# The FFN and its second products: six head units, units in pairs, operand sets in the order of use, outputs added from PSUM

## The chip, the cores and the metric

The kernel runs on one core of a Trainium2 chip. The time is the device time of one execution, in microseconds. Each core has five engines with instruction streams of their own that meet only through semaphores: PE (matrix products; its weight loads are shown as PEld), DVE (vector), ACT (activation), POOL (GpSimd) and SP, which here only issues DMAs.

## The reference

A block over a sequence of 1024 tokens with 1024 channels: a mixer (a gated convolution and a state-space scan, merged), then a SwiGLU feed-forward network (FFN), each behind a normalization that is shifted and scaled by a condition, then a last normalization.

```python
def ffn_sublayer(h, w_ffn_in, w_ffn_down):
    gate, up = jnp.split(h @ w_ffn_in, 2, axis=-1)
    return (jax.nn.silu(gate) * up) @ w_ffn_down
...
x = x + gate * mixer_sublayer(h, ...)
shift, scale, gate = adaln(c, w_ada_ffn[i], b_ada_ffn[i])
h = rms_norm(x, norm_ffn_w[i]) * (1.0 + scale) + shift
x = x + gate * ffn_sublayer(h, w_ffn_in[i], w_ffn_down[i])
return rms_norm(x, final_norm_w)
```

D_FF is 2816, so the FFN has 22 blocks of 128 gate and up columns.

## The kernel before

Channels lie on partitions (blocks of 128) and tokens in two halves of 512. Every fp32 operand is split into a high and a low part (`split`, `wsplit`): ACT writes the high part, then DVE or POOL subtracts it from the raw value for the low part. A product of four blocks is 12 matmuls (`mmp`, line 804).

Large products are done by units. A unit multiplies a 2x2 arrangement of weight blocks (two output blocks by two halves of the input channels) by a 2x2 arrangement of activations (two channel halves by the two token halves) in seven products instead of eight, as Strassen and Winograd do. The weights of products a to g are two blocks as they are, four combinations (`fs`, and three made in place, lines 901 to 906) and one more block. The activations are seven operand sets of four blocks each, made once for all units by `tok_ops`: B11 and B21 are the tiles H of the first token half as they stand; T1 to T4 and B22 come from `b2` (the second half), `t1` and `b21` (the first half, summed on POOL again from the parts of H by `whole`). `Unit.first` does the products a and b, which need only H. `Unit.rest` does the other five, in the order T1, T2, B22, T3, T4. Three accumulators take them: X, Y, Z in PSUM.

Three stages matter here:
- The FFN (`ffn_in`, 22 units, names `f0` to `f21`): `second` loads the second half, `tok_ops` normalizes it and makes the sets while the first `FF_HEAD` = 4 units do their products a and b. From then on a unit's `first` stands beside the `rest` of the one before. Results go to DRAM (`act_d`).
- The second products (`down_both(q)`, q = 0 and 1, four units each, names `d00` to `d13`): the same scheme on eight blocks of `act_d`; sets first, four `first`, then four `rest`. `Down.done` loads a block of x from DRAM (`pv`, two buffers), adds the product times the gate and stores it.
- The remainder (`down_rest`): six blocks without units, the last normalization, and the output.

The letters of `ENG_A`, `ENG_F`, `ENG_D` give the engine (v DVE, g POOL) of a unit's seven weight splits and its four weight combinations, for the first units and then for all others. Weight blocks arrive in 512 KB DMAs (`load_unit`: the first block of a unit in the tag `wraw`, the second in `fraw`, two buffers each). A head unit's first block is loaded twice: once for `first`, once for `rest`. The order on each engine is made by a scheduler from the order of the code and its own estimate of times; each engine, SP's queue among them, then works strictly in that order.

Of the kernel before, what the change touches and what calls it, by code (L numbers as in the profile page):

```python
# [14 lines left out]
P = 128  # L15
# [13 lines left out]
FF_HEAD = 4  # L29
FF_TAIL = 2  # L30
D_NEXT = 1
# [42 lines left out]
def build(tc, ins, outs):  # L74
# [208 lines left out]
    def bcast(colsr, name, far=True):  # L283
# [16 lines left out]
        bcast.last = last.ins  # L300
# [31 lines left out]
    row_d = dram.tile([24, NCK, P], F32, name="row_d")  # L332
    H = [tuple(hpool.tile([P, T], F32R, name=f"H{q}{k}") for q in "hl") for k in range(KD)]

    def make_h(k, t, gcol, shift, r, eng, dst=H):
        vec.scalar_tensor_tensor(out=t, in0=t, scalar=gcol[:, k:k + 1], in1=r, op0=ALU.mult, op1=ALU.mult)
        hi, lo = dst[k]
        act(out=hi, in_=t, func=AF.Identity, bias=shift[:, k:k + 1])
        if eng is vec:
# [446 lines left out]
    def load_unit(*cs):  # L786
        t = []
        for c in cs:
            if c != cs[0]:
                w = pools["u"].tile([P, 8 * P], F32, tag="fraw", name=f"fw{c}", bufs=2)  # L790
# [29 lines left out]
    def tok_ops(pool_, b2, t1, norm):  # L820
# [12 lines left out]
        for k in range(4):  # L833
            whole(t1[k], k)
# [14 lines left out]
        for k in range(4):  # L849
            less(k, t1[k])  # L850
            bsp("T1", k, t1[k], vec)
        for k in range(4):
            less(4 + k, t1[k])
            bsp("T2", k, t1[k], vec)
            bsp("B22", k, b2[4 + k], gp)
        for k in range(4):
            gp.tensor_tensor(out=b2[k], in0=b2[4 + k], in1=b2[k], op=ALU.subtract)
            bsp("T3", k, b2[k], vec)
        for k in range(4):
            b21 = tmp(f"b21_{k}")  # L860
            whole(b21, 4 + k)
# [17 lines left out]
    class Unit:  # L879


        def __init__(self, name, i, cons, four, engs):
            self.name, self.i, self.cons, self.four, self.engs = name, i, cons, four, engs

        def first(self, raw):
            n, e = self.name, self.engs
            self.raw = raw if len(raw) == 4 else None
            self.X = xtile(self.i, f"uX{n}") if self.four else mmtile(f"uX{n}")
            Y = pstile(f"uY{n}")
            mmp(self.X, wsplit(raw[0], f"a{n}", e[0]), BO["B11"])  # L890
            s1 = self.cons.tile11()
            act(out=s1, in_=self.X, func=AF.Copy)
            mmp(Y, wsplit(raw[1], f"b{n}", e[1]), BO["B21"])
            self.cons.c11(s1, Y)

        def rest(self, raw):
            n, e, X = self.name, self.engs, self.X
            a11, a12, a21, a22 = raw or self.raw
            tick()
            s1 = pools["u"].tile([P, T], F32, tag="fs", name=f"fs{n}", bufs=1)  # L900
# [3 lines left out]
            e[9].tensor_tensor(out=a11, in0=s1, in1=a11, op=ALU.subtract)  # L904
            w2 = wsplit(a11, f"d{n}", e[3])
            e[10].tensor_tensor(out=a12, in0=a12, in1=a11, op=ALU.subtract)
            Z = pstile(f"uZ{n}")
            mmp(Z, w1, BO["T1"])
            s5 = ev(f"s5{n}")
            act(out=s5, in_=Z, func=AF.Copy)  # L910
            mmp(X, w2, BO["T2"], False)
            s2 = ev(f"s2{n}")
            act(out=s2, in_=X, func=AF.Copy)
            mmp(Z, wsplit(a12, f"e{n}", e[4]), BO["B22"], False)
            self.cons.c12(s2, Z)
            mmp(X, wsplit(a21, f"f{n}", e[5]), BO["T3"], False)
            self.cons.c22(s5, X)
            mmp(X, wsplit(a22, f"g{n}", e[6]), BO["T4"], False)
            self.cons.c21(X)
# [4 lines left out]
    def run_units(name, units, HEAD, TAIL, four, engs, pre, after):  # L924
# [9 lines left out]
        def p37(i, load):  # L934
            step(U[i].rest, units[i][:2] if load else None)
            for f in after.get(i, ()):
                step(f)
# [3 lines left out]
        for i in range(HEAD - 1):  # L941
            p37(i, True)
        for i in range(HEAD, N - TAIL):
            p12(i, True)
            p37(i - 1, i == HEAD)
# [5 lines left out]
        for i in range(N - TAIL, N):  # L951
            p37(i, True)


    class Each:
# [23 lines left out]
    class ConvIn:  # L979
        def __init__(self, i):  # L980
            self.i = i
# [46 lines left out]
    class SsmIn:  # L1028
# [45 lines left out]
    def phase_a():  # L1074
# [38 lines left out]
        def begin(_):  # L1113
            popen("a1", "a1")
            pools["u"], pools["nev"] = mp, 6
            pt = [pools["c"].tile([P, NH * T + CW - 1], F32, tag="u", name=f"t1_{k}", bufs=2) for k in range(2)]
            t1 = [pt[k // 2][:, k % 2 * T:(k % 2 + 1) * T] for k in range(4)]
            tok_ops(pools["a1"], x1t, t1, norm_of(x1t, r_row, gmix, mod_m[:, 0:8]))
# [551 lines left out]
```

## Time and profile before

| what | value |
|---|---|
| runs | 2179.09, 2188.5, 2185.9 us (median 2185.9) |
| the profiled execution | 2181.88 us, span 2180.2 us |
| busy: PE, DVE, POOL, ACT | 1969.9, 1600.5, 1271.0, 974.0 us |
| granted clock of TensorE, mean | 0.957 |
| moved by DMA | 360.71 MB |

In the profile one instruction of a group is named by line, engine, operation and tile: L213 is the low part of an activation split, L783 that of a weight split, L804 a product's matmul, L922 the addition of a product to an SBUF tile, L1404 the addition to `pv`. Buffer numbers are left out of names. In the 40 slices a digit is the busy share in tenths, and a slice is 54.5 us; the first is slice 0.

### The profile page before, as it was taken

What the parts mean: (1) busy time and instruction counts of PE and PEld (TensorE: products, weight loads), DVE (VectorE), ACT (ScalarE), POOL (GpSimd) and SP (SyncE); (2) the same over time, 40 slices, a digit from 0 to 9 for tenths busy, and PEclk for the clock granted to TensorE, in tenths of its full rate; (3) what the DMA queues carried; (4) which work ended last, traced back from release to release, by engine and by line L of the source; (5) the groups of instructions that cost most, each with busy time, mean ns of one, the idle gap of its engine ahead of it and who ended that gap; (6) DMA issues with size and microseconds to landing.
All of it is one profiled execution on the core that took longest, in us unless ns stands there. A gap on an engine that the chain in (4) does not pass through costs nothing.

```text
span 2180.2 us, 26745 instructions
## 1 busy us (share of the span) xinstructions
PE 1969.9 (90%) x8802; PEld 1558.0 (71%) x8802; DVE 1600.5 (73%) x2195; ACT 974.0 (45%) x1814; POOL 1271.0 (58%) x938
## 2 busy tenths in 40 slices
PE   3889999999999797999889899977999999978997
PEld 3668678787877566777677687755888888756775
DVE  8878889968897979778688955567544345797845
ACT  3544344444446656545554542344333333443443
POOL 4668668878875755576555755565333334665411
PEclk9999999999999898999999999987999999999898
DMA  8223222323227866877888777742222222545663
GB/s 313 88 82 104 87 76 97 115 87 105 99 83 236 260 214 192 289 250 258 267 292 281 231 236 258 234 151 82 83 79 80 87 83 97 169 164 181 201 215 114
DMA packets 161227, 360.71 MB, mean 165 GB/s; under 512 B 18440, under 2 KB 18880, under 8 KB 161088
## 3 DMA queue, kind: packets, MB, share of 16 engines
q1 hardware_dynamic: 161088, 359.00, 49.6%
q8 instruction: 69, 1.13, 0.2%
q14 instruction: 70, 0.57, 0.1%
HBM read 275.80 MB, written 83.13 MB: 165 GB/s over the span
## 4 chain that ended last, share of the span: by engine, by line
PE 47%; DVE 24%; DMA 14%; issue 5%; ACT 2%; POOL 2%; SPq 1%; DVEq 0%; POOLq 0%; ACTq 0%
PE uXp L804 11%; PE uXf L804 10%; PE uZp L804 6%; PE uZf L804 4%; PE uYp L804 3%; DMA wa_f<-in 2%; PE uYf L804 2%; DMA M<-acs_d 2%; DMA x_d<-pv 1%; DVE wa_f L244 1%; DMA yl<-y_d 1%; PE p L182 1%; DVE gc L1045 1%; PE p L183 1%; DVE pcM L659 1%
## 5 line engine op out<-in xcount | busy, mean ns | idle before, releaser
L168 POOL TENSOR_TENSOR wl<-w,wh 128x512 fp32r<-128x512 f32 x198 | 285.4, 1451 | 221.0 <-ACT wh L166 176.9
L166 ACT ACTIVATE wh<-w 128x512 fp32r<-128x512 f32 x232 | 136.7, 606 | 122.4 <-DMA w<-in 59.7
L547 ACT ACTIVATE M<-M,dt_acs 128x128 f32<-128x128 f32 x256 | 80.9, 389 | 41.9 <-DMA M<-acs_d 41.8
L552 POOL TENSOR_TENSOR M<-M,cbm 128x512 f32<-128x512 f32 x48 | 68.8, 1443 | 48.0 <-ACT M L549 43.9
L659 DVE SCALAR_TENSOR_TENSOR pcM<-u,cw_eo,pcM 128x512 f32<-128x512 f32 x120 | 90.2, 752 | 2.7
L659 DVE SCALAR_TENSOR_TENSOR pcQ<-u,pc,pcQ 128x512 f32<-128x512 f32 x112 | 84.4, 753 | 3.0
L659 DVE SCALAR_TENSOR_TENSOR pcR<-u,pc,pcR 128x512 f32<-128x512 f32 x104 | 78.4, 754 | 2.8
L183 PE MATMUL s<-Hl,wh 128*128 128x512 f32 x192 | 77.2, 403 | 3.7 <-DVE Hl L213 3.7
L184 PE MATMUL s<-Hh,wl 128*128 128x512 f32 x192 | 77.7, 406 | 2.4 <-POOL wl L168 2.4
L182 PE MATMUL s<-Hh,wh 128*128 128x512 f32 x192 | 77.2, 406 | 0.1
L182 PE MATMUL p<-Hh,wh 128*128 128x512 f32 x144 | 59.1, 430 | 19.6 <-DVE xo L1026 10.8
L182 PE MATMUL p<-Oh,wh 128*128 128x512 f32 x144 | 60.7, 421 | 10.8 <-DVE xo L1026 10.8
L922 DVE TENSOR_TENSOR s2f<-s2f,uZf 128x512 f32<-128x512 f32 x22 | 15.1, 686 | 73.9 <-PE uZf L804 73.9
L183 PE MATMUL p<-Hl,wh 128*128 128x512 f32 x144 | 60.2, 419 | 6.0 <-DVE Hl L340 5.9
L901 POOL TENSOR_TENSOR fsf<-fw 128x512 f32<-128x512 f32 x22 | 34.9, 1588 | 50.4 <-DVE cf3l L783 3.3
L903 DVE TENSOR_TENSOR fw<-fw,fw 128x512 f32<-128x512 f32 x31 | 47.3, 1525 | 22.9 <-POOL fsf L901 19.0
L183 PE MATMUL p<-Ol,wh 128*128 128x512 f32 x144 | 59.9, 416 | 0.0
L184 PE MATMUL p<-Oh,wl 128*128 128x512 f32 x144 | 59.4, 414 | 0.0
L184 PE MATMUL p<-Hh,wl 128*128 128x512 f32 x136 | 56.7, 417 | 0.0
L1023 DVE SCALAR_TENSOR_TENSOR p<-pre,pc,p 128x512 f32<-128x512 f32 x72 | 53.8, 747 | 1.1 <-ACT p L1019 0.5
L244 DVE CUSTOM_DVE_ANT_0 wa_f<-wa_f,rw,as_f 128x512 f32<-128x512 f32 x24 | 31.3, 1302 | 29.9 <-DMA wa_f<-in 29.8
L184 PE MATMUL wo<-Oh,wl 128*128 128x512 f32 x128 | 50.6, 398 | 2.2 <-POOL wl L168 2.2
(3626 smaller groups left out, 7188.6 us busy)
## 6 DMA issues: line engine op xcount, KB each, us to landing
fw<-in SPq DMA_DIRECT2D x131, 512.0 KB, 3.4
w<-in SPq DMA_DIRECT2D x100, 512.0 KB, 4.9
M<-acs_d SPq DMA_DIRECT2D x64, 256.0 KB, 6.5
wa_f<-in SPq DMA_DIRECT2D x48, 256.0 KB, 3.9
wa_m<-in SPq DMA_DIRECT2D x16, 512.0 KB, 10.2
xs<-xbc_d SPq DMA_DIRECT2D x32, 256.0 KB, 4.6
E<-eac_d SPq DMA_DIRECT2D x64, 128.0 KB, 6.0
y<-z_d SPq DMA_DIRECT2D x32, 256.0 KB, 5.7
```

Source lines behind the costliest of these rows:

```text
L166: act(out=hi[:, :n], in_=raw, func=AF.Copy)
L168: eng.tensor_tensor(out=lo[:, :n], in0=raw, in1=hi[:, :n].bitcast(F32), op=ALU.subtract)
L182: nc.tensor.matmul(out=out, lhsT=whi[:, sl], rhs=rh, start=first and i == 0, stop=False)
L183: nc.tensor.matmul(out=out, lhsT=whi[:, sl], rhs=rl, start=False, stop=False)
L184: nc.tensor.matmul(out=out, lhsT=wlo[:, sl], rhs=rh, start=False, stop=last and i == n - 1)
L244: vec.tensor_tensor_reduce(out=w, in0=w, in1=c, scale=1.0, scalar=first, op0=ALU.mult, op1=ALU.add, accum_out=o)
L547: act(out=m[:, sl], in_=m[:, sl], func=AF.Relu, scale=-1.0, bias=acs[:, c * 32 + hd:c * 32 + hd + 1])
L552: (gp if e or hf == 0 else vec).tensor_tensor(out=self.M[e], in0=self.M[e], in1=cbm, op=ALU.mult)
L659: vec.scalar_tensor_tensor(out=pt if k < n - 1 else out or pt, in0=src(k), scalar=w(k), in1=pt, op0=ALU.mult, op1=ALU.add)
L804: nc.tensor.matmul(out=out, lhsT=l[:, sl], rhs=r, start=first and k == 0 and i == 0, stop=k == 3 and i == 2, skip_group_check=True)
L903: e[8].tensor_tensor(out=a21, in0=a11, in1=a21, op=ALU.subtract)
L1023: vec.scalar_tensor_tensor(out=pt, in0=pre[:, k:k + T], scalar=wc(k), in1=pt, op0=ALU.mult, op1=ALU.add)
```

## The change

- `FF_HEAD` is 6. The X of units 4 and 5 are taken from the PSUM tiles of Y and Z.
- Units go in pairs: `rest` is a generator that stops after each product, and `rests` takes a product of one unit and then of the other. The head's six units make three pairs, the last two units of the FFN one, and the units of `down_both` two per q. After each round `more_ops` makes the next operand set, so that the sets stand in the code between the products that use them.
- In these two stages B22 and the difference for T3 are made on DVE. The first half's blocks are not summed from H: in the FFN, phase B writes four of them to `t1f` with one more ACT instruction each, and `b21` is still summed; in `down_both` all eight are loaded from `act_d`.
- In the head units and in `down_both` all seven weight splits are on DVE and the four combinations on POOL.
- `Down` adds each product from PSUM straight into `pv` (`p1` to `p7`); the blocks of x are loaded when the unit's part begins. There are eight buffers for `pv` (tag `g0`).
- The last scaling of a half reads the broadcast row from PSUM on DVE; two of eight blocks stay on POOL.

```diff
-FF_HEAD = 4
+FF_HEAD = 6
-D_NEXT = 1
-N_PV = 2
+N_G0 = 8
-G_GP = 6
-ENG_F = ("ggggggggvvv", "ggvgvgvgvvv")
-ENG_D = ("gvvgggggvvv", "ggvgvgvgvvv")
+ENG_F = ("vvvvvvvgggg",) * 6 + ("ggvgvgvgvvv",)
+ENG_D = ("vvvvvvvgggg",)
...
     def make_h(...)
         act(out=hi, in_=t, func=AF.Identity, bias=shift[:, k:k + 1])
+        if keep is not None:
+            act(out=keep, in_=t, func=AF.Identity, bias=shift[:, k:k + 1])
...
     def tok_ops(...)
         for k in range(4):
             less(k, t1[k])
             bsp("T1", k, t1[k], vec)
+        yield
         for k in range(4):
             less(4 + k, t1[k])
             bsp("T2", k, t1[k], vec)
-            bsp("B22", k, b2[4 + k], gp)
+        yield
         for k in range(4):
-            gp.tensor_tensor(out=b2[k], in0=b2[4 + k], in1=b2[k], op=ALU.subtract)
+            bsp("B22", k, b2[4 + k], other)
+        yield
+        for k in range(4):
+            other.tensor_tensor(out=b2[k], in0=b2[4 + k], in1=b2[k], op=ALU.subtract)
             bsp("T3", k, b2[k], vec)
+        yield
...
+    def more_ops(gen=None):
+        if gen:
+            ops_left[:] = [gen]
+        if ops_left and next(ops_left[0], ops_left) is ops_left:
+            ops_left.clear()
+
+    def rests(us, raw):
+        gens = [u.rest(raw and raw[4 * i:4 * i + 4]) for i, u in enumerate(us)]
+        while gens:
+            gens = [g for g in gens if next(g, gens) is not gens]
+            more_ops()
...
     class Down:
-        def done(self, src, m, hf):
+        def begin(self, part):
+            for m, hf in ((0, 0),) if part == 0 else ((1, 1), (0, 1), (1, 0)):
+                t = self.t[m, hf] = pools["u"].tile([P, T], F32, tag="g0", ..., bufs=N_G0)
+                dma(out=t, in_=x1_d[hf, m + 2 * self.u])
+
+        def add(self, src, m, hf, last):
+            t = self.t[m, hf]
             m += 2 * self.u
-            t = pools["d0"].tile([P, T], F32, tag="pv", name=f"pv{self.q}{hf}_{m}", bufs=N_PV)
-            dma(out=t, in_=x1_d[hf, m])
             vec.scalar_tensor_tensor(out=t, in0=src, scalar=mod_f[:, 16 + m:17 + m], in1=t, op0=ALU.mult, op1=ALU.add)
-            dma(out=x1_d[hf, m], in_=t)
-
-        def c11(self, s1, Y):
-            add(s1, s1, Y)
-            self.done(s1, 0, 0)
+            if last:
+                dma(out=x1_d[hf, m], in_=t)
+
+        def p1(self, X):
+            self.add(X, 0, 0, False)
+
+        def p2(self, Y):
+            self.add(Y, 0, 0, True)
...
-                        (gp if k % 3 == 1 else vec).tensor_tensor(out=o, in0=o, in1=r, op=ALU.mult)
+                        (gp if k % 4 == 1 else vec).tensor_tensor(out=o, in0=o, in1=r if k % 4 == 1 else bcast.row,
+                                                                  op=ALU.mult)
```

How instructions move is seen at three places. First POOL at the head of the FFN, before, from the first split of a `df` on:

```order
L783 TENSOR_TENSOR df0l<-fw_12623,df0h 128x512
L783 TENSOR_TENSOR ef0l<-fw_12623,ef0h 128x512
L783 TENSOR_TENSOR ff0l<-fw_12625,ff0h 128x512
L857 TENSOR_TENSOR b2f_12350<-b2f_12358,b2f_12350 128x512
L213 TENSOR_TENSOR B22l_12417<-b2f_12358,B22h_12416 128x512
L857 TENSOR_TENSOR b2f_12352<-b2f_12360,b2f_12352 128x512
L783 TENSOR_TENSOR gf0l<-fw_12625,gf0h 128x512
```

The same engine there now, from the sums for `b21` on (`fsf` and `fw` are the weight combinations of units 0 and 1):

```order
L833 TENSOR_TENSOR b_0_12882<-Hh_111,Hl_112 128x512
L833 TENSOR_TENSOR b_1_12889<-Hh_113,Hl_114 128x512
L916 TENSOR_TENSOR fsf_12660<-fw_12608 128x512
L918 TENSOR_TENSOR fw_12608<-fw_12606,fw_12608 128x512
L919 TENSOR_TENSOR fw_12606<-fsf_12660,fw_12606 128x512
L925 TENSOR_TENSOR fw_12606<-fw_12606 128x512
L916 TENSOR_TENSOR fsf_12683<-fw_12612 128x512
```

Splits, B22 and T3's differences have left POOL, and the combinations, of which only `fs` was here, have come.

Second DVE at the start of q=0, before, where it takes in the first unit's products (`dg`, `uYd`):

```order
L922 TENSOR_TENSOR dg_15809<-dg_15809,uYd_15792 128x512
L862 TENSOR_TENSOR td_0_15677<-b_0_15761,td_0_15677 128x512
L838 TENSOR_TENSOR td_2_15679<-b2d_6_15673,td_2_15679 128x512
L213 TENSOR_TENSOR T2l_15716<-td_1_15678,T2h_15715 128x512
L1404 SCALAR_TENSOR_TENSOR pv_0_15828<-dg_15809,mod_f,pv_0_15828 128x512
```

And now:

```order
L784 TENSOR_TENSOR ad01l<-fw_15700,ad01h 128x512
L211 TENSOR_TENSOR T2l_15936<-t1f_99,T2h_15935 128x512
L1478 SCALAR_TENSOR_TENSOR pv_0_15703<-uXd_15702,mod_f,pv_0_15703 128x512
L784 TENSOR_TENSOR bd01l<-fw_15700,bd01h 128x512
L873 TENSOR_TENSOR t1f_99<-b_4_16098,t1f_99 128x512
L842 TENSOR_TENSOR t1f_100<-b2d_5_15670,t1f_100 128x512
L865 TENSOR_TENSOR b2d_1_15662<-b2d_5_15670,b2d_1_15662 128x512
```

The product goes from `uXd` into `pv` in one instruction, and weight splits (L784) and T3's differences (L865) stand between the sets' rows.

Third SP's queue in q=0, before, around a unit's reload of weights (`fw`):

```order
L793 DMA fw_15875<-in 128x1024
L1405 DMA x_d<-pv_0_15828 128x512
L1350 DMA act_d<-g_21_15312 128x512
L1403 DMA pv_4_15914<-x_d 128x512
L793 DMA fw_15918<-in 128x1024
L1405 DMA x_d<-pv_2_15871 128x512
```

And now, between the reloads for the first unit and for the second:

```order
L794 DMA fw_15823<-in 128x1024
L1473 DMA pv_2_15908<-x_d 128x512
L1430 DMA b2d_0_16396<-act_d 128x512
L1511 DMA b_7_16119<-act_d 128x512
L1430 DMA b2d_1_16398<-act_d 128x512
L1511 DMA b_4_16834<-act_d 128x512
L1430 DMA b2d_2_16400<-act_d 128x512
L1430 DMA b2d_3_16402<-act_d 128x512
L794 DMA fw_15827<-in 128x1024
```

Loads of the next q's second half (`b2d` with numbers from 16396, which take the buffers of this q's `b2d`) and of `b21` now stand ahead of the second unit's reload.

More of the change, by code (lines that the diff above doesn't have):

```diff
@@ L299, in bcast @@
                                     rhs=ident, start=True, stop=True, skip_group_check=True)
-        bcast.last = last.ins
+        bcast.last, bcast.row = last.ins, pr
         t = stp.tile([P, T], F32, tag="st", name="bc" + name)
@@ L818, in build, with tok_ops @@
     BO = {}
-    def tok_ops(pool_, b2, t1, norm):
+    def tok_ops(pool_, b2, t1, norm, first=None, other=gp):
         BO.update(B11=H[0:4], B21=H[4:8], T1=[], T2=[], T3=[], T4=[], B22=[])
@@ L831, in whole @@
             gp.tensor_tensor(out=t, in0=H[k][0].bitcast(F32), in1=H[k][1].bitcast(F32), op=ALU.add)
-        for k in range(4):
-            whole(t1[k], k)
+        if first is None:
+            for k in range(4):
+                whole(t1[k], k)
         def less(k, t):
@@ L854, in tok_ops @@
             bsp("T2", k, t1[k], vec)
-            bsp("B22", k, b2[4 + k], gp)
+        yield
         for k in range(4):
-            gp.tensor_tensor(out=b2[k], in0=b2[4 + k], in1=b2[k], op=ALU.subtract)
+            bsp("B22", k, b2[4 + k], other)
+        yield
+        for k in range(4):
+            other.tensor_tensor(out=b2[k], in0=b2[4 + k], in1=b2[k], op=ALU.subtract)
             bsp("T3", k, b2[k], vec)
+        yield
         for k in range(4):
-            b21 = tmp(f"b21_{k}")
-            whole(b21, 4 + k)
+            b21 = first and first(4 + k)
+            if not b21:
+                b21 = tmp(f"b21_{k}")
+                whole(b21, 4 + k)
             vec.tensor_tensor(out=t1[k], in0=b21, in1=t1[k], op=ALU.subtract)
@@ L932, in p12, with p37 @@
             step(U[i].first, units[i][:2] if whole else units[i][:1])
[L934 to L937, printed above, removed]
+        def p37(n, load):
+            us = n if isinstance(n, tuple) else (n,)
+            step(lambda raw: rests([U[i] for i in us], raw), sum((units[i][:2] for i in us), ()) if load else None)
+            for i in us:
+                for f in after.get(i, ()):
+                    step(f)
         for i in range(HEAD):
             p12(i, False)
-        for i in range(HEAD - 1):
-            p37(i, True)
+        if pairs:
+            for i in range(0, HEAD, 2):
+                p37((i, i + 1), True)
+        else:
+            for i in range(HEAD - 1):
+                p37(i, True)
         for i in range(HEAD, N - TAIL):
             p12(i, True)
-            p37(i - 1, i == HEAD)
+            if i > HEAD or not pairs:
+                p37(i - 1, i == HEAD)
         for i in range(N - TAIL, N):
@@ L950, in run_units @@
             step(pre)
-        for i in range(N - TAIL, N):
-            p37(i, True)
-    class Each:
+        for i in range(N - TAIL, N, 2):
+            p37((i, i + 1), True)
+    class Each(Sums):
         def __init__(self, name, done):
@@ L1357, in second @@
             dma(out=b2[k], in_=src[k0 + k])
-        return b2, [pools["d0"].tile([P, T], F32, tag="d", name=f"t{name}_{k}", bufs=4) for k in range(4)]
+        return b2
     def act_load(hf, i, hl):
@@ L1370, in begin @@
             popen("cv", "cv", space=PSUM)
[L1371 removed]
             fp = popen("f", "f")
[L1373 to L1374 removed]
+            pools.update(u=fp, nev=8, nfr=4, nfs=1)
+            b2 = second(x1_d[1], 0, "f")
             r = bcast(r_x1[1], "x1f1", far=False)
[L1376 removed]
+            more_ops(tok_ops(fp, b2, t1f, norm_of(b2, r, gffn, mod_f[:, 0:8], KD, True), lambda k: None, vec))
             bg_ada.append(late(ADA_LATE, ada(None, wada_ffn, range(8, 12), mod_f, gffn, "f")))
@@ L1426, in down_both, with first @@
         ch = lambda m: CH_FD + 3 * m + q
+        def first(k):
+            t = tmp(f"b21_{k}")
+            dma(out=t, in_=act_d[0, KD * q + k])
+            return t
         def begin(_):
-            b2, t1 = second(act_d[1], KD * q, f"d{q}")
-            tok_ops(pools["u"], b2, t1, None)
+            b2 = second(act_d[1], KD * q, f"d{q}")
+            for k in range(4):
+                dma(out=t1f[k], in_=act_d[0, KD * q + k])
+            more_ops(tok_ops(pools["u"], b2, t1f, None, first, vec))
         def pre(_):
@@ L1441, in down_both @@
             step(U[u].first, units[u][:1])
-        for u in range(4):
-            step(U[u].rest, units[u])
-            if u == D_NEXT:
+        for u in range(0, 4, 2):
+            step(lambda raw, u=u: rests(U[u:u + 2], raw), units[u] + units[u + 1])
+            if u == 0:
                 step(pre)
```

135 lines of the change are left out of this document (78 added, 57 removed).

## The prediction

> **What bounds the kernel now.** I read the page first (engine totals, then the slices), next stretches of the second half, then who waited for whom in the slow stretches, then single instructions there.
>
> ```profile
> span 2180.2 us, 26745 instructions
> PE 1969.9 (90%) x8802; PEld 1558.0 (71%) x8802; DVE 1600.5 (73%) x2195; ACT 974.0 (45%) x1814; POOL 1271.0 (58%) x938
> PE   3889999999999797999889899977999999978997
> DVE  8878889968897979778688955567544345797845
> POOL 4668668878875755576555755565333334665411
> DMA  8223222323227866877888777742222222545663
> ```
>
> PE is the busiest engine, but in the last third its row dips three times (slices 27 and 28, then 35 to 38), and in each dip DVE rises to 8 or 9 and POOL to 5 or 6. The dips are the head of the FFN (1428 to 1510 us) and the two second products, q=0 and q=1 (1880 to 2095). A table of stretches gives their size (columns: busy time and starts of PE, weight loads, DVE, ACT, POOL; granted clock; DMA share; GB/s):
>
> ```profile
> 1436.20:1446.20 10.00, 2.86 (x13) 2.02 (x12) 9.55 (x12) 1.14 (x3) 9.36 (x8) 0.75 0.96 353
> 1449.00:1500.40 51.40, 37.67 (x123) 26.12 (x121) 48.48 (x45) 28.86 (x50) 35.04 (x22) 0.74 0.09 31
> 1525.00:1850.00 325.00, 325.00 (x1420) 266.17 (x1419) 145.22 (x189) 121.59 (x204) 118.55 (x87) 1.00 0.25 85
> 1888.00:1950.00 62.00, 46.54 (x183) 35.69 (x182) 61.56 (x58) 26.97 (x49) 47.91 (x29) 0.92 0.45 156
> 1999.00:2043.00 44.00, 32.23 (x112) 23.57 (x111) 43.21 (x44) 20.55 (x38) 30.98 (x20) 0.81 0.45 150
> 1880.00:2094.60 214.60, 184.91 (x750) 144.69 (x749) 172.19 (x186) 82.72 (x149) 110.68 (x69) 0.94 0.57 190
> ```
>
> From 1525 to 1850 PE is never idle: 325.0 us for 1420 matmuls, 0.229 us each. That is the price of a matmul when nothing is late, and the change can win nothing there. From 1449 to 1500 only 123 matmuls start where 224 would fit, and DVE is busy 48.5 of 51.4 us. In 1888 to 1950 and 1999 to 2043 DVE is busy 61.6 of 62 and 43.2 of 44. So DVE bounds the dips.
>
> The instructions of the products alone (line 804):
>
> ```profile
> 1427.00:1496.00 69.00, 43.76 (x144) 30.79 (x145) 0.75 0.31 107
> 1496.00:1525.00 29.00, 26.11 (x107) 20.81 (x107) 0.94 0.37 115
> ```
>
> 251 of them from 1427.8 (the first) to 1525.0 are worth 57.5 us; with 3.5 us for the sums of squares and the broadcast the head loses 97.2-57.5-3.5 = 36 us. From 1880 to 2094.6, 750 matmuls are worth 171.7 us: the second products lose 43 us. Who PE waits for, in the head (three rows) and in q=0 (five):
>
> ```profile
> PE bx1f L298 <- DVE r_x L278: 7.3, 1, 7.3
> PE uXf L804 <- DVE T2l L213: 6.7, 3, 3.8
> PE uZf L804 <- DVE T1l L213: 6.2, 3, 3.0
> PE uZd L804 <- ACT cd01h L781: 3.5, 1, 3.5
> PE uYd L804 <- ACT bd02h L781: 3.1, 1, 3.1
> PE uXd L804 <- POOL dd00l L783: 1.7, 1, 1.7
> PE uZd L804 <- DVE cd00l L783: 1.7, 1, 1.7
> PE uZd L804 <- POOL ed00l L783: 1.4, 1, 1.4
> ```
>
> **The price of a DVE instruction.** It has two values:
>
> ```profile
> 1478.15 1.75 DVE L213 TENSOR_TENSOR T2l<-tf,T2h 128x512 fp32r<-128x512 f32 x1
> 1472.61 1.71 POOL L857 TENSOR_TENSOR b2f<-b2f,b2f 128x512 f32<-128x512 f32 x1
> 1887.74 1.28 DVE L838 TENSOR_TENSOR td<-b2d,td 128x512 f32<-128x512 f32 x2
> 1436.93 4.98 POOL L831 TENSOR_TENSOR tf<-Hh,Hl 128x512 f32<-128x512 f32 x4
> L1404 DVE SCALAR_TENSOR_TENSOR pv<-dg,mod_f,pv 128x512 f32<-128x512 f32 x8 | 10.4, 1301 | 0.0
> L1404 DVE SCALAR_TENSOR_TENSOR pv<-uXd,mod_f,pv 128x512 f32<-128x512 f32 x6 | 4.5, 749 | 7.6 <-PE uXd L804 6.7 <-DMA pv<-x_d 0.8
> ```
>
> Alone it takes 0.6 us from start to start (two in 1.28, the last one's tail included); beside a POOL instruction 1.75. The same instruction costs 1.30 with both tensors in SBUF, 0.75 with one in PSUM. What a POOL instruction adds comes from three stretches, as DVE's busy time less 0.6 per instruction: (48.5-45x0.6)/22 = 0.98, (61.6-58x0.6)/29 = 0.92, (43.2-44x0.6)/20 = 0.84. I take 0.92. The Trainium skill, "SBUF — State Buffer", section "SBUF: two separate sides", says that DVE with two SBUF inputs and GpSimd hold a shared port pair in turn, for the whole instruction. The trace agrees in kind. By that rule the charge would be POOL's whole 1.25 us (four in 4.98): 0.33 more on 13 and 20 instructions counted below, 11 us in all, so 2141 us instead of my sum; the three stretches decide for 0.92.
>
> **The change, part by part.**
>
> *Head of the FFN, set-up.* Before the sets can be made, twelve small DVE instructions (`rsqrt`) run from 1436.2 to 1446.2, beside POOL (9.36 us busy in the stretch quoted). At the end of the program the same chain runs without POOL, and there are the rows that set when set-making starts:
>
> ```profile
> 2164.84 0.16 DVE L270 TENSOR_SCALAR vx<-scx 128x4 f32<-128x4 f32 x1 [2.48 <-PE scx L259]
> 2167.02 0.16 DVE L278 SCALAR_TENSOR_TENSOR rx<-tx,rx 128x4 f32<-128x4 f32 x1
> 1449.04 0.75 DVE L872 SCALAR_TENSOR_TENSOR b2f<-b2f,gffn,bcx1f 128x512 f32<-128x512 f32 x1 [2.86 <-ACT bcx1f L302]
> 1452.45 0.63 ACT L781 ACTIVATE bf3h<-fw 128x512 fp32r<-128x512 f32 x1 [3.45 <-PE uYf L804]
> 1418.55 0.72 ACT L338 ACTIVATE Hh<-xh_x1f,mod_f 128x512 fp32r<-128x512 f32 x1 [4.89 <-DVE xh_x1f L336]
> fw<-in SPq DMA_DIRECT2D x131, 512.0 KB, 3.4
> ```
>
> Alone it is 2.3 us. The change takes POOL's four sums of H away from this place (phase B keeps them in `t1f`) and moves POOL's splits to DVE; two of POOL's other instructions still overlap it. I take 4.5 us for the chain, so the broadcast comes some 5 us earlier. DVE cannot use all of that: in its new order `bf3l` stands ahead of the first row of the sets, and `bf3h` waits for a weight buffer that the first Y frees. Set-making starts at about 1447 in place of 1449. The four kept copies are ACT instructions of 0.72 us in phase B, 2.9 us on an engine busy 45% of the span; taken at nothing, at worst 3.
>
> *Head of the FFN, sets.* From the first scaled `b2` to the last low part of T4 stand 62 DVE rows now (45 before, in 51.4 us), with 13 POOL instructions (22 before): 62x0.6 + 13x0.92 + 1 for the longer form = 50 us, to 1497. B22's and T3's work and all splits now stand on DVE, and the four weight sums of a unit on POOL. So the last set is ready only 3 us earlier than before. The gain is what PE has done by then. Two more units give it four more products, and each set feeds two products: its order has 242 product matmuls ahead of the first that waits for T4, where 144 had been started by 1496 before (row above). PE is through these at about 1498.5; that is 70.7 us for 55.4+3.5 us of work. With 2 us for the joints behind, the head loses 14 in place of 36: a gain of 22, which is also about what the 98 matmuls more are worth (98x0.229). Ends: 8, if DVE keeps the mean of the stretch, 48.5/45 = 1.08 us (62 rows, 67 us, 17 later); 30, if POOL's charge all but falls away (62x0.6, 1485).
>
> The next two pairs need ten products, 27.5 us of PE, against 18 DVE rows and 8 POOL ones, 18 us; a reload of a weight block (3.4 us) follows the fifth product's split and has 16 us before it is needed. Taken at nothing. From unit 6 on the order is the old one. The two extra reloads are 1 MB at a DMA share of 0.09: nothing.
>
> *Second products.* Removed per q: eight sums on POOL. Of the 28 DVE instructions that take products in, 12 read SBUF alone (1.30 in the row quoted) and now all 28 read PSUM (0.75). Added: eight loads, and B22, T3 and 28 weight splits on DVE; POOL keeps 16 instructions of some 37. From the first row of q=0's sets to its last split DVE has 131 rows, and 20 POOL ones lie beside them: 131x0.6 + 20x0.92 = 97 us. PE's order has 422 matmuls there, 97 us as well. With no slack, waits at the joints remain: I put the five waits quoted (11.4 us) back as 12. For q=1, 87 rows and 16 POOL ones make 67 us against 321 matmuls, 73.5 us, and its sets are made while q=0 still multiplies: joints 4. The loss is 16 in place of 43: a gain of 27. Ends: 10, if DVE keeps 172.2/186 = 0.93 us for its 218 rows (203 us for 170 us of PE); 37, if only q=1's kind of joints is left. DMA carries 4 MB more (16 loads of 256 KB) at a share of 0.57 that rises with the shorter time; in the slices of phase B (13 to 26) DMA stands at 7 or 8 and PE at 8 or 9, so nothing, at worst 5.
>
> *End.* The last scaling:
>
> ```profile
> 2142.32 6.41 DVE L1484 TENSOR_TENSOR x<-x,bcx 128x512 f32<-128x512 f32 x5 [1.22 <-ACT bcx L302]
> 2167.24 2.07 PE L298 MATMUL bx<-ident,rx 128*128 128x128 f32 x8 [2.43 <-DVE rx L278]
> 2169.35 0.60 ACT L302 ACTIVATE bcx<-bx 128x512 f32<-128x512 f32 x1 [5.56 <-PE bx L298]
> 2169.98 6.29 DVE L1484 TENSOR_TENSOR x<-x,bcx 128x512 f32<-128x512 f32 x5 [2.79 <-ACT bcx L302]
> ```
>
> DVE reads the broadcast from PSUM, so it starts 0.6 us sooner, and six instructions take 6x0.6 = 3.7 us in place of five in 6.29, with two left on POOL: 3 us at the end, 1 at the first half. A gain of 4 (2 to 6).
>
> *Phase A.* A few sets and splits change places at its head; no instruction is added. Nothing, 2 either way.
>
> **The sum.** 22+27+4 = 53 us off the profiled execution. Its time is 2181.9 (span 2180.2 and 1.7 around it), 4 below the median of 2185.9 and between the runs of 2179.1 and 2188.5. The forecast is 2129 us.
>
> **Rivals.**
> 1. *PE alone is left as the bound.* For it: PE's order has work for every wait of before. Against: 97 us of DVE against 97 of PE in q=0. Upper ends: 30+37+6 = 73, 2109 us.
> 2. *DVE stays the bound at its present mean.* For it: DVE rows rise by 17 in the head and 13 per q, and DVE obeys its order, so that a late load stops everything behind. Lower ends: 8+10+2 = 20, 2162 us.
> 3. *Slower: the reload of weights is held up on SP.* In q=0 SP issues the reload of the second unit behind loads of q=1's `b2`, which wait for DVE to finish T3; eight pairs (three in the FFN, one at its end, four in q=0 and q=1) have such a reload ahead of their weight sums. For it: SP issues in order. Against: a reload takes 3.4 us and has some 10 before its product. It decides from 53/8 = 6.6 us per pair; at 8 us the time is 2129+64 = 2193.
> 4. *No change*, a weaker case of the same, 5 to 7 us per pair: 2172 to 2190.
>
> **How the numbers follow.** Forecast 0.56, of its own range 2118 to 2142; PE-bound 0.17; DVE-bound 0.18; no change 0.05; slower 0.04. The range goes to the two ends of the first two rivals, 2107 to 2162. 0.5% (11 us) is about what a measurement of this kernel tells from no change: faster 0.91, same 0.05, slower 0.04.
>
> **What would show it.** In the changed profile: the `rsqrt` chain ahead of the FFN near 4.5 us; the last T4 split near 1497; DVE full until then, POOL at some 20 us, and some 240 product matmuls started; PE full from 1500 to the end of the FFN; waits of PE for DVE and ACT of some 16 us in q=0 and q=1 together; DVE rows with PSUM inputs at 0.75. Wrong would be: DVE rows at 1.75 through the head, SP's waits in front of weight reloads growing into waits of PE for POOL, or a stall of PE inside the first three pairs.

## The result, and the profile after

The changed kernel takes 2135.4 us (median of 4 runs, 2132.5 to 2138.0) against 2186.1 for the kernel before (4 runs, 2179.1 to 2188.5). The ratio is 0.9773, interval 0.9746 to 0.980. The forecast was 2129, range 2107 to 2162. The profiled execution took 2132.5 us: 49.4 less than that of before, where the sum said 53. One run of edit 10's kernel and one of the kernel before took more than twice as long and are left out of all figures.

The page of the changed kernel, engine totals and slices:

```profile
span 2130.5 us, 26723 instructions
PE 1954.8 (92%) x8802; PEld 1554.5 (73%) x8802; DVE 1561.3 (73%) x2242; ACT 964.2 (45%) x1792; POOL 1168.1 (55%) x871
PE   4879999999998889898989899998999999989997
DVE  8868889958899878959779783758644444598645
POOL 4568678887885854585655764555333333331410
```

PE's row has lost most of its dips: with the first slice as 0, slices 26 and 27 (the prediction calls them 27 and 28) had 7 and 7 and have 9 and 8, and slices 35 and 36 had 7 and 8 and have 8 and 9. POOL is busy 103 us less, DVE only 39 us less. Two rows date the parts (columns: count, shortest/median/longest ns, first and last start): the first product of the FFN and the first of the second products.

```profile
L805 PE MATMUL uXf<-Hh,af0h x4: 388/390/395, 1425.9 to 1429.2; 128*128 128x512 f32 x4
L805 PE MATMUL uXd<-Hh,ad00h x4: 389/390/395, 1863.7 to 1869.0; 128*128 128x512 f32 x4
```

Before, they stood at 1427.8 and 1888.2. So the FFN (first product to first second product) went from 460.4 to 437.8 us, 22.6 less; the rest, to the end of the span, from 292.0 to 266.8, 25.2 less; phases A and B gave 1.9. Every experiment below is measured by these two lengths beside its ratio. In the profiles of all the kernels run here the FFN's first product lies anywhere from 1423.4 to 1437.7, though few of the edits touch what is ahead of it, and executions of one kernel differ by as much (2136.9 to 2152.7 us in edit 4). A total therefore mixes in up to 14 us that cannot be put down to an edit in the FFN. The two lengths have a limit too: each is read from one execution.

Stretches of the changed kernel (columns as in the prediction's table): the making of the FFN's sets, and 90 and 100 us from the first second product on.

```profile
1446.70:1496.50 49.80, 41.51 (x162) 32.65 (x161) 47.35 (x61) 29.34 (x53) 27.06 (x13) 0.90 0.15 51
1863.70:1953.70 90.00, 80.66 (x336) 63.80 (x335) 85.68 (x122) 39.74 (x67) 26.08 (x16) 0.96 0.72 238
1953.70:2053.70 100.00, 97.68 (x416) 78.54 (x415) 61.18 (x89) 30.74 (x53) 21.98 (x15) 0.98 0.62 200
```

The same two stretches of the kernel before, from its own first second product:

```profile
1888.20:1978.20 90.00, 74.44 (x304) 58.25 (x302) 80.67 (x83) 36.56 (x66) 58.30 (x36) 0.94 0.51 171
1978.20:2078.20 100.00, 87.18 (x348) 68.16 (x349) 81.19 (x88) 38.69 (x69) 49.12 (x31) 0.91 0.56 189
```

In 190 us PE starts 752 matmuls in place of 652. At 0.229 us each the loss falls from 41 to 18 us, 13 of them in the first 90 us and 5 in the next 100. In the first 90 us DVE is still full (85.7 us), but it does 122 instructions there in place of 83, beside 16 POOL ones in place of 36. Who PE still waits for, in the head (three rows) and in the second products (three):

```profile
PE uZf L805 <- DVE B22l L211: 4.2, 1, 4.2
PE uZf L805 <- DVE g L985: 2.8, 2, 1.5
PE bx1f L296 <- DVE r_x L276: 1.8, 1, 1.8
PE uZd L805 <- DVE cd01l L784: 4.0, 1, 4.0
PE uXd L805 <- DVE dd10l L784: 2.1, 1, 2.1
PE uZd L805 <- DVE cd00l L784: 1.8, 1, 1.8
```

The head by the prediction's own measure, the product matmuls in 97.2 us from the first one on, before and now (the columns of PE and its weight loads alone):

```profile
1427.80:1525.00 97.20, 69.87 (x250) 51.42 (x250) 0.81 0.33 110
1425.90:1523.10 97.20, 83.90 (x343) 66.65 (x343) 0.95 0.40 141
```

At 0.229 us each, and with the same 3.5 us for the sums of squares and the broadcast, the head loses 15 us where it lost 36. Not all of that is waiting. PE is busy 69.9 us for 57.3 us of matmuls before, and 83.9 for 78.5 now. Behind its wait of 7.3 us for the broadcast in the kernel before, for instance, matmuls started 0.43 us apart (1448.6 to 1451.2) in place of 0.23, and from 1472 to 1492 the granted clock stood at 0.50. So up to 7 of the 21 us won are matmuls that run faster and not waits that are gone; no run varied the clock by itself.

### The profile page after: what moved, and what is told of

It is laid out like the page before. It is cut to its first block, busy times and chain, and to the rows that moved or that the text cites. A ratio compares the mean times of both kernels' runs of the same rounds, so it can differ in the third digit from the quotient of the medians.

```text
span 2130.5 us, 26723 instructions
## 1 busy us (share of the span) xinstructions
PE 1954.8 (92%) x8802; PEld 1554.5 (73%) x8802; DVE 1561.3 (73%) x2242; ACT 964.2 (45%) x1792; POOL 1168.1 (55%) x871
## 4 chain that ended last, share of the span: by engine, by line
PE 53%; DVE 23%; DMA 13%; issue 4%; ACT 3%; POOL 3%; SPq 1%; DVEq 0%; POOLq 0%; ACTq 0%
PE uXp L805 12%; PE uXf L805 10%; PE uZp L805 6%; PE uZf L805 5%; PE uYp L805 3%; PE uYf L805 2%; DMA M<-acs_d 2%; PE uXd L805 2%; DMA wa_f<-in 2%; DMA yl<-y_d 1%; DVE wa_m L242 1%; DVE wa_f L242 1%; DVE Hl L211 1%; PE uZd L805 1%; PE fd L180 1%
## 5 line engine op out<-in xcount | busy, mean ns | idle before, releaser
L918 POOL TENSOR_TENSOR fw<-fw,fw 128x512 f32<-128x512 f32 x40 | 58.0, 1450 | 117.5 <-DMA fw<-in 116.8
L916 POOL TENSOR_TENSOR fsf<-fw 128x512 f32<-128x512 f32 x22 | 41.2, 1873 | 65.3 <-DVE cf2l L784 10.8
L180 PE MATMUL p<-Hh,wh 128*128 128x512 f32 x144 | 59.0, 430 | 19.1 <-DVE xo L1097 10.8
L985 DVE TENSOR_TENSOR s2f<-s2f,uZf 128x512 f32<-128x512 f32 x22 | 15.1, 687 | 62.5 <-PE uZf L805 62.5
L925 POOL TENSOR_TENSOR fw<-fw 128x512 f32<-128x512 f32 x40 | 58.6, 1466 | 1.5
L180 PE MATMUL wo<-Oh,wh 128*128 128x512 f32 x128 | 51.6, 403 | 0.0
```

The lines of the kernel that those rows point to most:

```text
L180: nc.tensor.matmul(out=out, lhsT=whi[:, sl], rhs=rh, start=first and i == 0, stop=False)
L918: e[8].tensor_tensor(out=a21, in0=a11, in1=a21, op=ALU.subtract)
```

## The experiments

The theory at the start was the prediction's: DVE bounds the dips, a POOL instruction beside it costs it 0.92 us, and what PE can do before the last set is ready ("cover") decides how much of that is lost. The rivals: the splits' place alone makes the gain, or the sums, or the PSUM adds. Each edit is to the changed kernel unless it says otherwise. A ratio is to runs of the kernel before on the same chip; their medians lie between 2182 and 2188 us, so ratios compare better than times. For stretches of which an edit leaves the code as it is, the profiles differ by some us: from the first second product to the end 266.8, 265.7, 263.2 and 266.5 us in four kernels (mean 265.6), the FFN 437.8, 437.6 and 439.6 in three.

**1. Four head units.**

```diff
-FF_HEAD = 6
+FF_HEAD = 4
-(True, (4, 5)), engs_f
+(True, ()), engs_f
```

> The changed kernel with four head units in place of six. Theory (cover): two units fewer take four products, 48 matmuls or 11 us of PE, away from ahead of the first product that waits for T4; DVE is spared six rows there (four splits, two sums, 3.6 us). Net 7 to 8 us slower than the changed kernel: about 2143 us, ratio to the kernel before 0.980 to 0.982. Rival 1 (the two units are the whole gain of the head): 20 to 22 us slower, 2156, ratio 0.986 or more. Rival 2 (PE ran out of nothing, the sets just came earlier): no change, 2135, ratio 0.977.

2143.2 us, ratio 0.9798 (0.978 to 0.9815). The FFN takes 442.6 us, 4.8 more; the first product lies 6 us later, which the edit does not explain. The theory holds in kind, with 5 us in place of 7 or 8; the two units are not the whole gain of the head.

**2. The head's units one after the other.**

```diff
-            for i in range(0, HEAD, 2):
-                p37((i, i + 1), True)
+            for i in range(HEAD):
+                p37(i, True)
```

> The changed kernel with the six head units of the FFN finished one after the other in place of in pairs product by product; the second products keep their pairs. Theory (cover): only one unit's four products lie ahead of T4, 48 matmuls or 11 us less, and DVE's rows are the same: 11 us slower than the changed kernel, 2146 us, ratio 0.981 to 0.984. Also more waits at each joint between sets, since a set feeds one product of 2.75 us before the next set is needed: up to 5 us more. Rival (the sets are made in 50 us whatever PE does, and PE has its work later instead): under 3 us, ratio 0.978 or less.

2135.8 us, ratio 0.976 (0.9741 to 0.978); the FFN takes 437.6 us, as before the edit. The rival's result, and the splits of T4 say why. Those of the changed kernel and of this one:

```profile
L211 DVE TENSOR_TENSOR T4l<-t1f,T4h x4: 683/684/685, 1493.4 to 1495.8; 128x512 fp32r<-128x512 f32 x4
```

```profile
L211 DVE TENSOR_TENSOR T4l<-t1f,T4h x4: 680/680/682, 1489.8 to 1491.6; 128x512 fp32r<-128x512 f32 x4
```

Counted from each kernel's own first product (1425.9 and 1429.1) the last one starts after 69.9 and after 62.5 us. With one unit ahead, the second unit's weight splits and sums stand behind the sets: from the first product to the last T4 split there are 80 DVE rows and 14 POOL instructions in place of 83 and 17. So T4 is ready 7.4 us earlier; that nearly pays for 11 us less of cover. The expectation had "DVE's rows are the same", which was wrong: cover and the rows that it costs come together.

**3. The old tables of engines.**

```diff
-ENG_F = ("vvvvvvvgggg",) * 6 + ("ggvgvgvgvvv",)
-ENG_D = ("vvvvvvvgggg",)
+ENG_F = ("ggggggggvvv", "ggvgvgvgvvv")
+ENG_D = ("gvvgggggvvv", "ggvgvgvgvvv")
```

> The changed kernel with the old tables of engines in the FFN and its second products: of a unit's seven weight splits four go back to POOL, and of its four weight sums three to DVE; net one instruction more on POOL and one less on DVE per unit. Theory (charge of 0.92 us on DVE per POOL instruction against 0.6 for the row on DVE): 0.3 us per unit, 2 us in the head and 3 in the second products, plus waits of PE for splits that stand in POOL's queue at 1.3 to 1.6 us each: 5 us slower in all (2 to 12), ratio 0.978 to 0.983. Rival (the splits' place is the main gain of the change): 20 us slower or more, ratio 0.986 or more.

2147.7 us, ratio 0.9811 (0.9794 to 0.9828). The FFN takes 443.3 us (5.5 more), the rest 267.4 (1.8 over the mean, hardly beyond what unedited ones differ by); the start of the FFN, 11 us later, is again not the edit's. Within what the theory gave; not the main gain.

**4. B22 and T3 back on POOL.**

```diff
-more_ops(tok_ops(fp, b2, t1f, ..., lambda k: None, vec))
+more_ops(tok_ops(fp, b2, t1f, ..., lambda k: None, gp))
-more_ops(tok_ops(pools["u"], b2, t1f, None, first, vec))
+more_ops(tok_ops(pools["u"], b2, t1f, None, first, gp))
```

> The changed kernel with the splits of B22 and the differences of T3 back on POOL (eight instructions in the head, eight per second product). Theory: DVE loses eight rows (4.8 us) and is charged eight times 0.92 (7.4 us) in each of the three places, 2.6 us each where DVE is full; POOL's queue, which also holds the weight sums, gets 8 x 1.3 to 1.6 us longer, 11 us, which the pair's next weight sums wait behind: 8 us slower in all (3 to 20), ratio 0.978 to 0.986. Rival (DVE's row count is what bounds, as the full 50 us of the head): 24 rows fewer give 5 to 14 us back, ratio 0.975 or less.

2146.0 us, ratio 0.9804 (0.977 to 0.9838). The FFN takes 444.2 us (6.4 more), the rest 267.6 (2.0 over the mean, again hardly beyond that). The four splits of B22 now take 1.7 us each on POOL, yet the last ends 63.6 us after the FFN's first product, where in the changed kernel it ended after 63.4. PE no longer waits for B22, but it waits 5.8 us for ACT's copies of Z (`s5f`), and the last split of T4 starts after 72.7 us in place of 69.9. Fewer rows on DVE gained nothing, so the rival falls.

**5. The second products' units one after the other.**

```diff
-        for u in range(0, 4, 2):
-            step(lambda raw, u=u: rests(U[u:u + 2], raw), units[u] + units[u + 1])
-            if u == 0:
+        for u in range(4):
+            step(lambda raw, u=u: rests(U[u:u + 1], raw), units[u])
+            if u == 1:
                 step(pre)
```

> The changed kernel with the units of the second products finished one after the other in place of in pairs; the FFN keeps its pairs. Theory (cover): in q=0 48 matmuls or 11 us fewer lie ahead of the last set while DVE's rows are the same, in q=1 the sets are early anyway: 8 to 13 us slower than the changed kernel, ratio 0.981 to 0.984. Rival (PE's few waits there come from weight sums and not from sets): under 3 us either way, ratio 0.976 to 0.979.

2129.9 us, ratio 0.9758 (0.9736 to 0.9779). From the first second product to the end it is 259.6 us, 7.2 less than in the changed kernel and 6.0 below the mean: neither the theory nor the rival. The ratio alone does not tell this from the changed kernel, but edit 12 shows the short length a second time. So the pairs cost time here. The wait of 4.0 us for `cd01l`, the second unit's split, is gone; one of 4.8 us for `dd00l` stands in its place:

```profile
PE uXd L805 <- DVE dd00l L784: 4.8, 1, 4.8
PE uZd L805 <- DVE pv L1478: 3.2, 2, 2.1
PE uZd L805 <- ACT cd01h L782: 0.5, 1, 0.5
```

All of PE's waits in the 190 us fall only from 11.5 to 8.8 us; where the rest of the time goes is not shown.

**6. The kernel before with DVE's and POOL's work exchanged, and nothing else of the change.**

```diff
-ENG_F = ("ggggggggvvv", "ggvgvgvgvvv")
-ENG_D = ("gvvgggggvvv", "ggvgvgvgvvv")
+ENG_F = ("vvvvvvvgggg",) * 6 + ("ggvgvgvgvvv",)
+ENG_D = ("vvvvvvvgggg",)
-            bsp("B22", k, b2[4 + k], gp)
+            bsp("B22", k, b2[4 + k], vec if norm is None or norm[2] else gp)
...
-            gp.tensor_tensor(out=b2[k], in0=b2[4 + k], in1=b2[k], op=ALU.subtract)
+            (vec if norm is None or norm[2] else gp).tensor_tensor(out=b2[k], in0=b2[4 + k], in1=b2[k], op=ALU.subtract)
```

The condition holds in the FFN and its second products; phase A keeps `gp`.

> The kernel before with one part of the change alone: the tables of engines (seven splits of a unit on DVE, four weight sums on POOL) and B22's splits and T3's differences on DVE; four head units, no pairs, old order of sets, old adds. Theory (the port's charge buys little, the cover of PE is the gain): in the head 17 rows more on DVE at 0.6 and 9 POOL instructions less at 0.92 all but cancel, 2 us longer; in the second products 13 rows more and some 12 POOL instructions less per q, 3 us shorter each: within 6 us of the kernel before, ratio 0.997 to 1.003. Rival (taking POOL out of DVE's way is the gain): 20 us or more faster, ratio 0.991 or less.

2162.3 us, ratio 0.9907 (0.9878 to 0.9936): 20 us faster, as the rival said. The FFN takes 450.1 us (10.3 less than before), the rest 280.7 (11.3 less). My expectation had miscounted: 6 of the 17 rows more in the head belong to the two extra units, which this kernel does not have. Its head, in the table's columns:

```profile
1449.50:1496.50 47.00, 36.92 (x132) 26.20 (x131) 42.88 (x56) 29.12 (x51) 22.28 (x11) 0.86 0.10 34
```

56 rows and 11 POOL instructions for 45 and 22, in 47.0 us for 51.4. The price of the prediction gives 56x0.6 + 11x0.92 = 43.7 us; the row says 42.9. So the price held and the count in the expectation did not. Seen from PE, the waits for `T2l` fall from 6.7 to 2.2 us and those for `T1l` from 6.2 to 5.0. What makes the other 6 of the 10.3 us was not taken apart; the granted clock of the stretch rose from 0.74 to 0.86.

**7. A second buffer for a unit's weight sum,** taken for odd units from the ring of output buffers.

```diff
-            s1 = pools["u"].tile([P, T], F32, tag="fs", name=f"fs{n}", bufs=pools["nfs"])
+            s1 = pools["u"].tile([P, T], F32, name=f"fs{n}", **(dict(tag="g0", bufs=N_G0) if self.four[0] and self.i % 2 else dict(tag="fs", bufs=pools["nfs"])))
```

> The changed kernel with a second buffer for a unit's first weight sum (odd units take theirs from the buffers of the outputs), so that POOL can make the second unit's sum of a pair before the first one's low part is split. Theory (joints): in the changed kernel POOL waits 3.7 us in the head and 3.8 in q=0 for that buffer, its sum then takes 7.71 us beside DVE's unbroken rows, and PE waits 4.2 us for B22 behind it and 4.0 us for the split of the second sum in q=0; both go or halve: 4 to 8 us faster than the changed kernel, ratio 0.973 to 0.9755. Rival (DVE is full and obeys its order, so the sets come no earlier): under 2 us, ratio 0.976 to 0.979.

2157.6 us, ratio 0.9882 (0.986 to 0.9904). The FFN gains 1.2 us and the rest loses 19.5. Waits in the second products, of POOL, then of PE:

```profile
POOL fsd L916 <- DMA x_d<-pv: 24.0, 3, 12.6
POOL fsd L916 <- DVE pv L1478: 16.2, 1, 16.2
PE uZd L805 <- ACT cd01h L782: 13.8, 1, 13.8
PE uZd L805 <- ACT cd03h L782: 6.6, 1, 6.6
```

The ring gives its buffers in order, so the sum waits until an output tile ahead of it is added to and stored, and PE waits for the sum. That is a fault of the edit, which put one wait for another. A spare buffer of its own was not tried.

**8. The last two sums of H for T4 on DVE.**

```diff
-        def whole(t, k):
-            gp.tensor_tensor(out=t, in0=H[k][0].bitcast(F32), in1=H[k][1].bitcast(F32), op=ALU.add)
+        def whole(t, k, e=gp):
+            e.tensor_tensor(out=t, in0=H[k][0].bitcast(F32), in1=H[k][1].bitcast(F32), op=ALU.add)
...
-                whole(b21, 4 + k)
+                whole(b21, 4 + k, gp if k < 2 or first is None else vec)
```

> The changed kernel with the last two sums of H for T4 in the head (two instructions) on DVE in place of POOL. Theory: DVE no longer waits 2.45 us for POOL's sum, which itself waited for the 7.71 us sum of weights; 1.2 us of rows are added; the splits of B22, for which PE waits 4.2 us, come some 4 us earlier: 2 to 5 us faster than the changed kernel, ratio 0.975 to 0.9765, and in the profile no wait of DVE for POOL there and a wait of PE for B22 under 1 us. Rival: PE's work ahead of T4 ends at the same time, since T4's last split comes no earlier: no change in time, the wait only moves.

2131.9 us, ratio 0.9767 (0.9748 to 0.9785), which by itself is not told from the changed kernel's. The FFN takes 434.4 us, 3.4 less (unedited ones differ by 2.0), and PE's wait for B22 is gone. POOL's row in the two kernels, the changed one and this:

```profile
1473.47 7.71 POOL L916 TENSOR_TENSOR fsf<-fw 128x512 f32<-128x512 f32 x1 [3.69 <-DVE cf1l L784]
```

```profile
1478.88 17.35 POOL L916 TENSOR_TENSOR fsf<-fw 128x512 f32<-128x512 f32 x1 [3.70 <-DVE cf1l L784]
```

The same sum takes 1.3 us elsewhere. It ends 1.2 us after DVE's unbroken run of SBUF instructions ends (1480.0 and 1495.1), and nothing on DVE waits for POOL any more, so the run goes on longer.

**9. Sums of H on POOL again.**

```diff
-               t1f[k] if keep and k < 4 else None)
+               None)
-tok_ops(fp, b2, t1f, ..., lambda k: None, vec)
+tok_ops(fp, b2, t1f, ..., None, vec)
-            for k in range(4):
-                dma(out=t1f[k], in_=act_d[0, KD * q + k])
-            more_ops(tok_ops(pools["u"], b2, t1f, None, first, vec))
+            more_ops(tok_ops(pools["u"], b2, t1f, None, None, vec))
```

> The changed kernel with the sums of H for T1 and T4 made again by POOL in all three places: no copies kept in phase B (four more POOL instructions ahead of the FFN's sets), and eight POOL sums per second product in place of eight loads. Theory A (each POOL instruction that lies beside full DVE costs it 0.92 us, and a sum that is late holds the set): from the first FFN product to the first second product 4 to 9 us longer than the changed kernel's 437.8 us, mostly by a longer rsqrt chain (4.5 us back to some 8 or 10) and a later T1; from there to the end 8 to 15 us longer than its 266.8; together 12 to 24 us, ratio 0.983 to 0.988. Rival B (the sums were hidden, the gain of the second products is that of the adds and the splits): under 5 us, ratio 0.976 to 0.9795.

2141.7 us, ratio 0.9793 (0.9759 to 0.9827). The FFN takes 440.2 us (2.4 more, hardly beyond the spread), the rest 270.9 (5.3 over the mean): between the two theories, and by the ratio not told from rival B. The `rsqrt` chain stayed at 4.4 us. With `t1f` in place since phase B, the four sums were made before the FFN, so this run does not put POOL's work back beside the chain.

**10. Products copied from PSUM before they are added.**

```diff
+            s = tmp(f"ps{self.q}{hf}_{m}")
+            act(out=s, in_=src, func=AF.Copy)
-            vec.scalar_tensor_tensor(out=t, in0=src, ...
+            vec.scalar_tensor_tensor(out=t, in0=s, ...
```

> The changed kernel with each product of the second products first copied from PSUM to SBUF by ACT (56 copies more) and added from there by DVE. Theory A (an add that reads PSUM escapes POOL): the adds beside POOL go from 0.75 to 1.3 or more; with 16 POOL instructions per q that is at most 16 of 56, 9 us of DVE, of which half on the path; with the copies' own delay ahead of each joint 3 to 10 us slower than the changed kernel from the first second product on, ratio 0.978 to 0.982. Rival B (the PSUM adds carry most of the second products' gain that the engine tables alone left, 25.2 less 11.3 us): 12 us slower or more, ratio 0.983 or more. Rival C: PSUM is freed sooner by the copy, and nothing is lost: under 2 us.

2149.4 us (3 runs), ratio 0.983 (0.9794 to 0.9867). From the first second product on it is 277.7 us, 12.1 over the mean and 10.9 over the changed kernel: between theory A and rival B. The adds, here and in the changed kernel (two rows):

```profile
L1480 DVE SCALAR_TENSOR_TENSOR pv<-ps,mod_f,pv 128x512 f32<-128x512 f32 x55 | 53.1, 970 | 0.1
```

```profile
L1478 DVE SCALAR_TENSOR_TENSOR pv<-uXd,mod_f,pv 128x512 f32<-128x512 f32 x32 | 24.0, 748 | 11.2 <-PE uXd L805 11.2
L1478 DVE SCALAR_TENSOR_TENSOR pv<-uZd,mod_f,pv 128x512 f32<-128x512 f32 x16 | 11.9, 745 | 0.2 <-PE uZd L805 0.2
```

The 0.22 us more is a mean of two values. 44 of the 56 adds take 0.75 us as before, and 12 of the 15 that lie beside a POOL instruction take 1.7 to 1.9: 12 us of DVE. In the changed kernel 14 adds lie beside a POOL instruction, and all take 0.75. So an add that reads PSUM does escape POOL, as theory A says. But PE also waits 10.1 us for the copies that the edit added; what the PSUM adds are worth without the copies was not measured.

**11. All sets written out at once.**

```diff
-        if ops_left and next(ops_left[0], ops_left) is ops_left:
-            ops_left.clear()
+        while ops_left:
+            if next(ops_left[0], ops_left) is ops_left:
+                ops_left.clear()
```

> The changed kernel with all operand sets of a place written out at its start, as in the kernel before, in place of one set per product. Theory A (the order written decides what DVE does first, and sets come ahead of the splits of the head units): the last T4 split comes earlier, but low parts of weights for the first products come later and PE stalls there: 3 to 8 us slower in the FFN's head and 3 to 8 in the second products, ratio 0.980 to 0.984. Rival B (the order is set by data and priorities, not by where a set is written): under 3 us either way, ratio 0.976 to 0.979.

2138.9 us, ratio 0.9768 (0.9732 to 0.9805). The FFN takes 436.5 us, the rest 263.5. Rival B: where a set is written makes no difference that can be seen.

**12. Edits 5 and 8 together.**

> The changed kernel with the two edits that shortened a part in the profiles joined: the last two sums of H for T4 in the head on DVE (434.4 us from the first FFN product to the first second product, against 437.8), and the units of the second products one after the other (259.6 us from there to the end, against 266.8). Theory (the two parts are apart in the program and add up): 3 + 7 = 10 us faster than the changed kernel, about 2125 us, ratio 0.970 to 0.9745. Rival (parts of the program ahead of them vary by as much from kernel to kernel and hide it, or the 7 us were one execution's): ratio 0.9755 to 0.9775.

2125.0 us (6 runs, 2118.2 to 2130.0), ratio 0.9715 (0.9689 to 0.9742), below the changed kernel's whole interval. The FFN takes 434.6 us and the rest 257.9, as the two had alone. By its ratio the version beats both kernels, the changed one narrowly.

## Why the prediction was right, point by point

- **What bounds the dips.** Right. DVE is busy 47.35 of 49.8 us while the head's sets are made, and 85.7 of 90 us in q=0.
- **The price of a DVE instruction.** Right, and a little high. 0.6 us a row and 0.92 per POOL instruction give 61x0.6 + 13x0.92 = 48.6 us for the head (47.35 measured) and 122x0.6 + 16x0.92 = 87.9 for q=0's 90 us (85.7). Worked back, the charge per POOL instruction is 0.83 us in the head, 0.78 in q=0 and 0.84 in edit 6. At POOL's whole 1.25 us (four in 4.98), the charge by the rule of the Trainium skill, "SBUF — State Buffer", section "SBUF: two separate sides", the head would be 52.9, which the trace does not bear out. The charge is a mean only: one POOL sum waited 7.7 us and cost DVE's rows beside it nothing.
- **Head, set-up.** The `rsqrt` chain runs from 1434.3 to 1438.8, 4.5 us as forecast, and the unbroken run of the sets' rows starts at 1446.8 (forecast 1447). Edit 6, which leaves POOL's four sums where they were, has 10 us.
- **Head, sets.** The last split of T4 starts at 1495.8 (forecast: ready at 1497), and POOL's row shows 27 us there, not 20, of which some 6 are one sum's waiting (edit 8). By 1496 some 225 product matmuls had started, not 240, since PE waited 4.2 us for B22: 81 more than before and not 98. The loss is 15 us against 14, and the FFN's gain 22.6 against 22. The size was right, the account of it only in part, and so the near hit is partly luck. The text let the two more units and the pairs win nearly all of it, as cover; undone alone, the head units are worth 4.8 us, the pairs nothing (edits 1 and 2). The engines' exchange alone is worth 10.3 in the kernel before, a part to which the text gave no size of its own, and 5.5 and 6.4 by its two halves in the new one.
- **Second products.** The step "joints 12 and 4" was near: the loss over 190 us is 18 against 16, and PE's waits there are 11.5 us. It was 41 before by the same measure, so the gain is 23, against 27. "Back as 12" took pairs for a help; edits 5 and 12 show that they cost some 7 us, so here too the near hit is partly luck. DMA's share rose to 0.72 and no wait of PE for a load shows there, as taken.
- **End.** Mis-sized: 1.6 us at the end in place of 3. The row of the last scaling:

```profile
2121.90 3.68 DVE L1566 TENSOR_TENSOR x<-x,bx 128x512 f32<-128x512 f32 x6 [2.79 <-ACT bcx L300]
```

  The six rows take 3.7 us, as worked out. But they start after ACT's copy all the same (2.79 us idle, as before), and the span ends 4.9 us behind the last of them, where before it ended 3.9 behind. The 2.1 MB of output stores now run without a break at some 380 GB/s. The 1 us at the first half was not measured by itself.
- **Phase A.** 1.9 us earlier, inside the 2 either way.
- **Rivals.** 1 did not come: DVE still bounds q=0. 2 was too slow by 27 us. 3, a held-up reload on SP, did not show: PE's waits in the second products end with splits on DVE and ACT, none with a reload. Edit 7 shows its cousin at full size, a buffer that comes free late and costs 20 us.
- **Signs.** PE is busy 363.0 of the 363.7 us from 1500 to the first second product, and the adds that read PSUM take 0.75 us, as forecast. Three figures of the text are slightly off without weight: the rival price gives 2140 us and not 2141, the lower end of the range is 2109 by its own sum and not 2107, and the first dip is in slices 26 and 27.

In the FFN, parts undone one at a time cost 4.8 + 5.5 + 6.4 + 2.4 = 19.1 of the 22.6 us, each read from one execution and good to some 2 us; parts that overlap need not add up. In the second products the same edits give 1.8 + 2.0 + 5.3 and 12.1 with the copies' own cost, less 7 for the pairs, against 23 to 25; how these share the gain stays open. That the exchange of engines is worth 11.3 there in the kernel before and some 4 in the new one suggests that they overlap. Two parts of the change were undone by no run: four buffers in place of two for the second weight block (`fraw`), and the last two scalings of `b2`, which went from POOL to DVE.

## What to carry to other kernels

Count a full DVE by its rows and by the POOL instructions beside it together: moving an instruction from POOL to a full DVE cost 0.6 us and gave 0.8 to 0.9 back on the mean, and the waits behind POOL's queue went with it. More work ahead of a late set is worth less than its length, because its own splits stand on the same engine ahead of that set; in the second products the pairs even cost some 7 us. Measure an edit by the length of its own part of the program, between two instructions that every version has, when the parts ahead of it wander by more than the effect.

## What the runs showed of the hardware

A POOL instruction can be held up for as long as DVE's run lasts. A sum that takes 1.3 us elsewhere took 17.34 us in the kernel of edit 12, while DVE did SBUF instructions at 0.6 us each with no gap. It ended at 1490.29, 1.2 us after the run, which is about its own length. Behind the run DVE was idle for 0.49 us and then read PSUM; in the changed kernel the 7.71 us sum ended 1.2 us after a run with idle time alone behind it, so an idle gap is enough. POOL's row, then DVE's last of the run and the first behind it:

```profile
1472.95 17.34 POOL L916 TENSOR_TENSOR fsf<-fw 128x512 f32<-128x512 f32 x1 [3.69 <-DVE cf1l L784]
```

```profile
1487.25 1.88 DVE L211 TENSOR_TENSOR T4l<-t1f,T4h 128x512 fp32r<-128x512 f32 x3
1489.62 1.29 DVE L985 TENSOR_TENSOR s2f<-s2f,uZf 128x512 f32<-128x512 f32 x2 [0.49 <-PE uZf L805]
```

So a POOL instruction in such a run is free for DVE and late for whoever waits for it, as the 2.5 us that DVE itself waited for the sum of H in the changed kernel. The other way, eight of twelve DVE instructions of 128x4 that take 0.16 us alone took 0.9 to 1.2 us while POOL's stood back to back (edit 6). The same section of the Trainium skill says that whoever starts first holds the pair for its whole instruction while the other is blocked; the 1.2 us, about one POOL instruction (1.26 us), agree with it, and the 17.34 us add that DVE's next instruction can come ahead of a POOL one that has been waiting.
